# Four-head and half-array TensorE products rewritten as products on the whole array, in a hybrid decoder step

## The chip, the cores and the metric

The kernel runs as one program on one core of a Trainium2 chip. The metric is device time of one execution in microseconds (us); the kernel before has a median of 2491.27 us over three runs (2490.3 to 2497.3).

## The reference

One inference step of a two-layer trunk over 560 token columns: 8 sample sequences of 4 tokens, 16 meta tokens and 512 prompt tokens, model width 1024, all in float32. Per layer:

```python
x = x + 0.5 * swiglu(rmsnorm(x, ffn1_norm), ...)          # 1024 -> 2*2816 -> 1024
h = rmsnorm(x, mix_norm);  parts = split(h @ w_mix_in)
fox  : 4 heads x 64, q/k rmsnorm, logits + F_q - F_k (F = cumsum of log forget gates), softmax
ssd  : conv + silu, 8 heads x 64, 2 groups of B/C; y = (C.B * exp(seg)) x + C h exp(cs)
gla  : 4 heads, key 32, value 64; glog = log_sigmoid(glr @ w_gate + bias) / 16
       att[t,s] = sum_k q[t,k] k[s,k] exp(b[t,k] - b[s,k]);  o = att v + (q exp(b)) S
x = x + concat(fox, ssd, gla) @ w_mix_out
x = x + 0.5 * swiglu(rmsnorm(x, ffn2_norm), ...)
```

The new keys, values, log forget gates and states are outputs too.

## The kernel before

Activations lie with features on the 128 partitions and tokens along the columns, in two groups: A (304 columns: 48 sample and meta tokens as tile 4, prompt tiles 0 and 1) and B (256 columns: prompt tiles 2 and 3). Large products are done in three float32r products of split operands (`mm3`: high by high, high by low, low by high); in the profile these are the matmuls with `hhi`, `hlo` or `hid` and `whi`, `wlo` or `keep`. Weights come in 512 KB pieces (`raw`), ScalarE rounds them to `whi`, VectorE (or now and then GpSimd) takes the rest as `wlo`. Products in plain float32 stand in the trace as two matmul records each.

Each layer runs FFN1, the mixing stage (`mix`), FFN2. In the mixing stage `MIX_ORDER` names the steps in the order of issue, and a scheduler in the language's tile framework lays them side by side: the projections (`fox_in`, `gla_in`, `ssd_in`, `out`) fill TensorE (PE) while the small steps of the head groups (`gla_tile`, `ssd_tile`, `fox_tile`, `fox_decode`, `fox_meta`, `fox_norm`) run between them. PE takes its instructions strictly in the order that the scheduler wrote.

The steps that the change touches:

- `gla_tile` (five tiles a layer) computes the decayed attention by levels: products between the two halves of a block of 128, of 64, of 32, 16 and 8 tokens. The four heads have 32 key rows each, so a head's product contracts over 32 of the 128 partitions (`zk[hr, ...]`, `zq[hr, ...]`). Heads are looped over; every head takes a PSUM bank, and its results go into `att` by ScalarE copies (two coarse levels) and by `copy_predicated` under a mask (three fine levels).
- `ssd_tile`: C by B (`gm`) and C by state (`pi`) are done for each of two groups on 64 of the partitions; the decay sums `pd` on 64 columns.
- `fox_norm`: each token tile's running sum of log forget gates is a product with 4 output rows, chained from tile to tile through `lsum`.
- `fox_tile`: the 16 meta keys are their own 16-row transpose (`femt`) and 16-row product with `Vm`; for the last tile, whose 528 keys don't fit a bank, the scores are cut 16 + 512.
- `gla_in`: the low-rank gate goes tile by tile through a 16-row transpose and a product that contracts over 16 rows.
- `norm`: eight squares; GpSimd adds the first seven, and two one-column products with `ones` for each token tile add the last.

Of the kernel before, what the change touches and what calls it, by code (L numbers as in the profile page):

```python
# [76 lines left out]
TM = [("gv", [(C_GV, 256), (C_GLR, 16)]), ("fv", [(C_FV, 256), (C_FF, 4)]),  # L77
# [9 lines left out]
def constants():  # L87
# [14 lines left out]
    same = seq[:, None] == seq[None, :]  # L102
    put("ident", np.eye(128))
# [4 lines left out]
    put("tri4", same & (t4[:, None] <= t4[None, :]))  # L108
# [11 lines left out]
    put("bd", (P // 32)[:, None] == (np.arange(256) // 64)[None, :])  # L120
    put("fsel", np.where((P // 64)[:, None] == np.arange(2)[None, :], 1.0 / 64, 0.0))
# [104 lines left out]
class Trunk:  # L226
# [108 lines left out]
    def setup_rest(self):  # L335
# [37 lines left out]
        self.Vm = self.t([16, 256], "Vm", pool=self.pers)  # L373
# [3 lines left out]
    def layer_params(self, l, pc=None):  # L377
# [7 lines left out]
        wg = self.t([16, 128], "wgate", pool=self.pers)  # L385
        nc.sync.dma_start(out=wg, in_=a["wgate"][l])
# [44 lines left out]
    def first_norm(self, g, gain):  # L431
# [19 lines left out]
        for j, (_, o, tn) in enumerate(tiles):  # L451
            for i in range(2):
                self.mm(ps[:tn, j:j + 1], acc[i][:, o:o + tn], self.c("ones")[:, 0:1], start=i == 0, stop=i == 1)
        r = self.norm_factors(ps, tiles)
        y = self.ps(pool)[:, :n]
        for j, (_, o, tn) in enumerate(tiles):
            self.tr(y[:, o:o + tn], r[:tn, j:j + 1].to_broadcast([tn, 128]))
# [4 lines left out]
    def norm_factors(self, ps, tiles):  # L462
        r = self.t([128, 2, 3], "nr", bufs=2, pool=self.tmp)
        nt = len(tiles)
        if nt == 3:
            self.V.memset(r[:, 0, 0:1], 1.0)
            self.V.tensor_scalar(r[:48, 0, 0:1], ps[:48, 0:1], 1.0 / D, EPS, op0=ALU.mult, op1=ALU.add)
        self.V.tensor_scalar(r[:, 0, nt - 2:nt], ps[:, nt - 2:nt], 1.0 / D, EPS, op0=ALU.mult, op1=ALU.add)
        return self.rpow(r[:, 0, :nt], r[:, 1, :nt])

    def norm(self, g, gain, order=range(8)):
# [13 lines left out]
        for j, (_, o, tn) in enumerate(tiles):  # L485
            self.mm(ps[:tn, j:j + 1], acc[:, o:o + tn], self.c("ones")[:, 0:1], stop=False)
            self.mm(ps[:tn, j:j + 1], sq[:, o:o + tn], self.c("ones")[:, 0:1], start=False)
        r = self.norm_factors(ps, tiles)
        y = self.ps(pool)[:, :n]
        for j, (_, o, tn) in enumerate(tiles):  # L490
            self.tr(y[:, o:o + tn], r[:tn, j:j + 1].to_broadcast([tn, 128]))
# [115 lines left out]
    def fox_in(self, l, H):  # L607

        for g in GRP:
# [3 lines left out]
            if g == "A":  # L613
                self.G.memset(R["lf"], 0.0)
                self.G.memset(R["fst"], 1.0)

        def use(g):
            def f(j, ti, c0, tn, ps):
                self.act(self.Vt[ti], ps[:tn, 0:256])
                if ti == 4:  # L620
                    self.act(self.Vm, ps[32:48, 0:256])
# [10 lines left out]
        for name in ("fk0", "fk1", "fq0", "fq1"):  # L632
# [4 lines left out]
            for g in GRP:  # L637
# [7 lines left out]
                for j, (ti, c0, tn) in enumerate(TILES[g]):  # L645
                    o = 8 * j + i + (24 if g == "B" else 0)
                    self.mm(pst[:tn, o:o + 2], sq[:, c0:c0 + tn], self.c("fsel"))
        for g in GRP:
            fst, o = self.R[g]["fst"], 24 if g == "B" else 8
            if g == "A":  # L650
                self.V.tensor_scalar(fst[:48, 0, :], pst[:48, 0:8], EPS, None, op0=ALU.add)
            nt = len(TILES[g])
            self.V.tensor_scalar(fst[:, nt - 2:nt, :], pst[:, o:o + 16].rearrange("p (j i) -> p j i", j=2), EPS, None, op0=ALU.add)

    def gla_in(self, l, g, H):
        R, n, nt = self.R[g], GRP[g][1], len(TILES[g])
        gin = self.g2(128 * nt).rearrange("p (j c) -> p j c", j=nt)
        if nt == 3:
            self.G.memset(gin[:, 0, :], 0.0)

        def use(j, ti, c0, tn, ps):
            gv = R["gv", ti] = self.t([128, 256], f"gv{j}")[:tn]
            self.act(gv, ps[:tn, 0:256])
            glr[j] = self.t([128, 16], "glr", bufs=3)[:tn]
            self.act(glr[j], ps[:tn, 256:272])

        glr = {}
        self.tok_unit(l, 0, g, H, use)
        for j, (ti, c0, tn) in enumerate(TILES[g]):
            pt = self.ps(self.psg)  # L670
            self.tr(pt[:16, :tn], glr[j])
            gt = self.t([16, 128], "glrT")
            self.act(gt[:, :tn], pt[:16, :tn])
            pg = self.ps(self.psg)
            self.mm(pg[:tn, :128], gt[:, :tn], self.wgate)
            self.tt(gin[:tn, j, :], pg[:tn, :128], self.row["gb"][:tn], ALU.add)
# [94 lines left out]
    def fox_norm(self, l, g):  # L771
# [7 lines left out]
        for j, (ti, c0, tn) in enumerate(tiles):  # L779
            e = self.f2(512)[:tn]  # L780
            self.act(e.rearrange("p (h d) -> p h d", h=8), y[:tn, j, :].unsqueeze(2).to_broadcast([tn, 8, 64]))
            ps = self.ps(self.psF)
            for i in range(4):
                self.tr(ps[:, i * tn:(i + 1) * tn], e[:, 128 * i:128 * i + 128])
            for h2 in range(2):
                pv = ps[64 * h2:64 * h2 + 64, :4 * tn].rearrange("p (a b t) -> p a b t", a=2, b=2)
# [12 lines left out]
        for j, (ti, c0, tn) in enumerate(tiles):  # L799
            lf = R["lf"][:tn, j, :]  # L800
            tri = self.c("tri") if tn == 128 else self.c("tri4")
            ps = self.ps(self.psF)
            self.mm(ps[:4, :tn], lf, tri[:, :tn], stop=ti == 4)
            if ti < 4:
                self.mm(ps[:4, :tn], self.lsum, self.c("ones")[:, :tn], start=False)
            fr = self.t([4, 128], "frow")
            self.act(fr[:, :tn], ps[:4, :tn], scale=-1.0)
            self.nc.sync.dma_start(out=self.kaug[64:65, :, c0g + c0:c0g + c0 + tn], in_=fr[:, :tn])
            if ti == 4:
                self.V.memset(self.lsum, 0.0)  # L810
                self.V.tensor_copy(self.lsum[32:48], lf[32:48])
            elif ti < 3:
                self.tt(self.lsum, self.lsum, lf, ALU.add)
# [18 lines left out]
    def fox_tile(self, g, i, c0):  # L832
# [3 lines left out]
        cut = 16 if kc + 16 > 512 else 0  # L836
        po = self.ps(self.psF)
        for hp in range(2):
            ets = []
            for h in (2 * hp, 2 * hp + 1):  # L840
                q = self.qaug[:, h, GRP[g][0] + c0:GRP[g][0] + c0 + 128]
                s = self.ps(self.psF)
                nk = kc + 16 - cut
                if cut:
                    sm = self.ps(self.psF)
                    self.mm(sm[:, 0:16], q, self.kaug[:, h, 32:48])
                self.mm(s[:, :nk], q, self.kaug[:, h, 32 + cut:48 + kc], stop=False)
                self.mm(s[:, nk - 128:nk], self.c("ident_b"), self.c("cmask_r"), start=False)
                sums = self.t([128, 2], "fsum", bufs=4)
                e = self.softmax_rows([s[:, :nk]] + ([sm[:, 0:16]] if cut else []), sums)  # L850
                if cut:
# [4 lines left out]
                em = e[1] if cut else e[0][:, 0:16]  # L856
                ek = e[0] if cut else e[0][:, 16:]
                pt = self.ps(self.psF)
                for k in range(i + 1):
                    self.tr(pt[:, 128 * k:128 * k + 128], ek[:, 128 * k:128 * k + 128])  # L860
# [5 lines left out]
                self.act(emt, pm[:16, :128]) if h % 2 else self.V.tensor_copy(emt, pm[:16, :128])  # L866
# [599 lines left out]
```

## Time and profile before

| | us |
|---|---|
| median of three runs | 2491.27 |
| the profiled execution | 2489.21 |
| its span (first to last instruction) | 2487.4 |
| PE busy | 2423.8 (97%) |
| VectorE (DVE) busy | 1243.0 (50%) |
| ScalarE (ACT) busy | 878.5 (35%) |
| GpSimd (POOL) busy | 505.5 (20%) |
| mean granted TensorE clock | 0.975 |

PE's busy time is a model: matmuls are pipelined, and a record lasts longer than the time after which the next one starts. So for PE the distance between starts is read, not the length of a record. "x12" in a timeline row is twelve records merged. The granted clock is 1.0 (2.4 GHz) or 0.5 (1.2 GHz) at any moment. The mixing stages lie at about 430 to 880 us and 1680 to 2090 us.

### The profile page before, as it was taken

What the parts mean: (1) busy time and instruction counts of PE and PEld (TensorE: products, weight loads), DVE (VectorE), ACT (ScalarE), POOL (GpSimd) and SP (SyncE); (2) the same over time, 40 slices, a digit from 0 to 9 for tenths busy, and PEclk for the clock granted to TensorE, in tenths of its full rate; (3) what the DMA queues carried; (4) which work ended last, traced back from release to release, by engine and by line L of the source; (5) the groups of instructions that cost most, each with busy time, mean ns of one, the idle gap of its engine ahead of it and who ended that gap; (6) DMA issues with size and microseconds to landing.
All of it is one profiled execution on the core that took longest, in us unless ns stands there. A gap on an engine that the chain in (4) does not pass through costs nothing. (4 is left out here: it accounts for less than half of the span.)

```text
span 2487.4 us, 45892 instructions
## 1 busy us (share of the span) xinstructions
PE 2423.8 (97%) x18346; PEld 2293.9 (92%) x18346; DVE 1243.0 (50%) x2747; ACT 878.5 (35%) x1990; POOL 505.5 (20%) x675
## 2 busy tenths in 40 slices
PE   8999999999999999999999999999999999999999
PEld 7999999987777899999999999999876779999999
DVE  5434344487687633333343333343867875333333
ACT  4323233444354432322333232334444544323221
POOL 3202124131232310110131010132322323101010
PEclk8999999998898999999999999999989999999999
DMA  4222223353331322222322222223523313222222
GB/s 148 87 88 87 90 84 88 106 146 96 98 95 53 115 69 85 87 86 88 98 67 85 87 86 86 83 90 105 156 87 106 94 58 110 86 85 85 86 86 87
DMA packets 89463, 230.61 MB, mean 93 GB/s; under 512 B 12482, under 2 KB 37826, under 8 KB 89250
## 3 DMA queue, kind: packets, MB, share of 16 engines
q1 hardware_dynamic: 88818, 227.53, 29.3%
q8 instruction: 144, 2.36, 0.4%
q14 instruction: 69, 0.57, 0.1%
q10 hardware_dynamic: 432, 0.16, 0.0%
HBM read 219.71 MB, written 7.92 MB: 92 GB/s over the span
## 5 line engine op out<-in xcount | busy, mean ns | idle before, releaser
L270 DVE TENSOR_TENSOR wlo<-raw,whi 128x512 fp32r<-128x512 f32 (+1 forms) x649 | 464.5, 720 | 404.1 <-ACT whi L276 395.8
L276 ACT ACTIVATE whi<-raw 128x512 fp32r<-128x512 f32 (+1 forms) x680 | 426.6, 630 | 657.7 <-PE ps L263 609.8
L263 PE MATMUL ps<-hhiA,wlo 128*128 128x304 f32 x1664 | 510.8, 307 | 0.0
L263 PE MATMUL ps<-hloA,whi 128*128 128x304 f32 x1664 | 510.2, 307 | 0.0
L263 PE MATMUL ps<-hhiA,whi 128*128 128x304 f32 x1664 | 510.0, 306 | 0.0
L263 PE MATMUL ps<-hhiB,wlo 128*128 128x256 f32 x1664 | 473.0, 285 | 2.4 <-DVE wlo L270 2.4
L263 PE MATMUL ps<-hhiB,whi 128*128 128x256 f32 x1664 | 472.1, 284 | 3.1 <-ACT s L276 2.5
L263 PE MATMUL ps<-hloB,whi 128*128 128x256 f32 x1664 | 470.6, 283 | 0.0
L263 PEld LDWEIGHTS ps<-hhiB,whi 128*128 128x128 f32 x1664 | 316.8, 190 | 7.7 <-ACT s L276 3.4
L263 PEld LDWEIGHTS ps<-hhiA,wlo 128*128 128x128 f32 x1664 | 316.7, 190 | 6.3 <-issue 4.7
L263 PEld LDWEIGHTS ps<-hhiB,wlo 128*128 128x128 f32 x1664 | 316.9, 190 | 5.1 <-DVE wlo L270 3.0
L263 PEld LDWEIGHTS ps<-hhiA,whi 128*128 128x128 f32 x1664 | 316.4, 190 | 4.9 <-issue 3.5
L263 PEld LDWEIGHTS ps<-hloA,whi 128*128 128x128 f32 x1664 | 317.3, 191 | 3.4 <-issue 2.4
L263 PEld LDWEIGHTS ps<-hloB,whi 128*128 128x128 f32 x1664 | 316.4, 190 | 1.7 <-issue 1.2
L270 POOL TENSOR_TENSOR hidA<-s,hidA 128x304 fp32r<-128x304 f32 x88 | 76.4, 868 | 849.3 <-ACT hidA L276 849.2
L263 PE MATMUL ps<-hidA,whi 128*128 128x304 f32 x1072 | 226.2, 302 | 0.0
L273 DVE SCALAR_TENSOR_TENSOR x<-ps,x 128x304 f32<-128x304 f32 (+1 forms) x192 | 85.9, 449 | 232.4 <-PE ps L263 230.6
L263 PE MATMUL ps<-hidB,whi 128*128 128x256 f32 x1072 | 195.2, 282 | 0.0
L263 PEld LDWEIGHTS ps<-hidA,whi 128*128 128x128 f32 x1072 | 174.4, 188 | 0.0
L263 PEld LDWEIGHTS ps<-hidB,whi 128*128 128x128 f32 x1072 | 166.3, 189 | 0.0
L270 DVE TENSOR_TENSOR s<-s,ps 128x256 f32<-128x256 f32 (+3 forms) x194 | 90.4, 466 | 149.5 <-PE ps L263 141.6
L263 PE MATMUL ps<-hidA,wlo 128*128 128x304 f32 x536 | 162.1, 302 | 0.0
(338 smaller groups left out, 3606.2 us busy)
## 6 DMA issues: line engine op xcount, KB each, us to landing
raw<-win SPq DMA_DIRECT2D x176, 512.0 KB, 3.3
raw<-wout SPq DMA_DIRECT2D x64, 512.0 KB, 3.5
raw<-wfm SPq DMA_DIRECT2D x48, 512.0 KB, 3.6
raw<-wmo SPq DMA_DIRECT2D x32, 512.0 KB, 3.6
raw<-wout SPq DMA_DIRECT2D x32, 384.0 KB, 3.7
pg<-kpage SPq DMA_DIRECT2D x64, 130.0 KB, 2.4
pg<-vpage SPq DMA_DIRECT2D x64, 128.0 KB, 2.3
raw<-wtm SPq DMA_DIRECT2D x8, 544.0 KB, 3.8
```

The lines of the kernel that those rows point to most:

```text
L263: return self.T.matmul(out, lhsT, rhs, start=start, stop=stop, **k)
L270: return (eng or self.V).tensor_tensor(out=out, in0=a, in1=b, op=op)
L273: return self.V.scalar_tensor_tensor(out=out, in0=a, scalar=s, in1=b, op0=op0, op1=op1)
L276: return self.S.activation(out, in_, f, **k)
```

## The change

Small products are padded or stacked to use all 128 rows and, where it can be, all 128 columns. For the levels of `gla_tile`, the four heads' q is laid side by side with zeros outside its own 32 rows (`qm`, from `hsel`), so one product over 128 rows with 512 columns gives all four heads in one bank; `qm` and one of the level operands are made on GpSimd, the others on VectorE. The masked copies then take four heads at once. `ssd_tile` does the same for two groups (`scz`, from `gsel`). Norms, forget sums, gates and meta keys use whole tiles, and the last square of a norm is now added by VectorE. The last FoX tile is cut 400 + 128. Pools change: `g2` 5 to 8 buffers, `pg` (cache pages) 12 to 10.

```diff
-ON_POOL = ["gdq1", "gpr3", "gqk", "gzq2", "sr1", "sst", "sy"]
-BUFS = {"s1": 5, "f2": 3, "g2": 5, "s2": 5, "pg": 12}
+ON_POOL = ["gqm", "gdq1", "gpr3", "gqk", "gzq2", "sr1", "sst", "sy"]
+BUFS = {"s1": 5, "f2": 3, "g2": 8, "s2": 5, "pg": 10}
...
 norm:
-            elif i < 7:
-                self.tt(acc[:, :n], acc[:, :n], sq[:, :n], ALU.add, self.G)
+            else:
+                self.tt(acc[:, :n], acc[:, :n], sq[:, :n], ALU.add, self.G if i < 7 else self.V)
-            self.mm(ps[:tn, j:j + 1], acc[:, o:o + tn], self.c("ones")[:, 0:1], stop=False)
-            self.mm(ps[:tn, j:j + 1], sq[:, o:o + tn], self.c("ones")[:, 0:1], start=False)
+            self.mm(ps[:, j:j + 1], acc[:, o:o + 128], self.c("ones")[:, 0:1])
...
 fox_norm (was five tiles, each chained through lsum):
+        self.mm(ps[:, 0:128], lw[:, 0, :], self.c("tri"), stop=False)
+        self.mm(ps[:, 0:48], lw[:, 2, :], self.c("tri4"), start=False, stop=False)
+        self.mm(ps[:, 0:128], lw[:, 1, :], self.c("ones"), start=False)
...
 fox_tile:
-                self.tr(pm[:16, :128], em)
-                emt = self.t([16, 128], "femt", bufs=2)
+                self.tr(pm[:, :128], e[0][:, 0:128])
+                emt = self.t([128, 128], "femt", bufs=2)
...
 ssd_tile:
-            self.mm(pg[:n, :n], bT[pr, cs], cT[pr, cs])
-            self.tt(gm[:, g2, :], pg[:n, :n], tri[:, :n])
+        self.tt(cz, cT[:, cs].unsqueeze(1).to_broadcast([128, 2, n]), self.c("gsel").unsqueeze(2).to_broadcast([128, 2, n]), eng=self.e("scz"))
+        self.mm(pg[:n, :2 * n], bT[:, cs], cz.rearrange("p g t -> p (g t)"))
-                self.mm(pi[:n, 0:256], cT[pr, cs], self.Ssd[pr, :])
+                self.mm(pi[:, 256 * g2:256 * g2 + 256], cz[:, g2, :], self.Ssd)
...
 gla_tile:
-            zq, zk = times(e[:, 0:w], q, f"gzq{lv[-1]}"), times(e[:, 0:w], k, f"gzk{lv[-1]}")
-            for h in range(4):
-                    self.mm(pa[:64, 0:64], zk[hr, 0:64], zq[hr, 64:128])
-                        self.mm(pa[b:b + 32, 64:96], zk[hr, o:o + 32], zq[hr, o + 32:o + 64])
-                        self.mm(pa[:n, ms], zk[hr, ms], zq[hr, ms])
-                        V.copy_predicated(out=att[:, h, :], mask=masks["lev"][:, m, :], data=pa[:n, i * n:(i + 1) * n])
+        self.tt(qm, q.unsqueeze(1).to_broadcast([128, 4, n]), self.c("hsel").unsqueeze(2).to_broadcast([128, 4, n]), eng=self.e("gqm"))
+            self.mm(pa[:, 0:256], zk[:, 0:n], z0)
+            self.mm(pa[:, 256:512], zk[:, n:2 * n], z1)
+            self.tt(zq.rearrange("p (h t) -> p h t", h=4), z.unsqueeze(1).to_broadcast([128, 4, n]), qm, eng=self.e(f"gzq{i}"))
+            self.mm(pa[:n, :4 * n], kk, zq)
+            V.copy_predicated(out=att, mask=masks["lev"][:, i, :].unsqueeze(1).to_broadcast([n, 4, n]),
+                              data=pa[:n, :4 * n].rearrange("p (h t) -> p h t", h=4))
```

The first place is PE in the first layer, at the levels of prompt tile 1 of `gla_tile` (`g` by `g` are level products, `pg` by `f` cache values in `fox_decode`, `hhiA` and `hloA` a projection). Before, three of the four heads at the coarse levels:

```order
L263 MATMUL ps_7028<-g_1135_7015,g_1136_7017 64x64
L263 MATMUL ps_7028<-g_1135_7015,g_1136_7017 32x32 x2
L263 MATMUL ps_7028<-g_1135_7015,g_1136_7017 128x128
L263 MATMUL ps_6992<-c_hsel_652,gpr_7079 128x4 x2
L263 MATMUL ps_7434<-hloA_4664,whi_7430 128x304
L263 MATMUL ps_7037<-g_1135_7015,g_1136_7017 64x64
L263 MATMUL ps_7037<-g_1135_7015,g_1136_7017 32x32 x2
L263 MATMUL ps_7037<-g_1135_7015,g_1136_7017 128x128
L263 MATMUL ps_6992<-c_hsel_652,gpr_7079 128x4
```

And now, on the same engine, the whole tile's levels:

```order
L265 MATMUL ps_6941<-g_1122_6942,g_1120_6939 128x256
L265 MATMUL ps_6941<-g_1123_6945,g_1120_6939 128x256
L265 MATMUL ps_6593<-pg_6649,f_995_6587 32x256
L265 MATMUL ps_6593<-pg_6647,f_995_6587 32x256
L265 MATMUL ps_6593<-pg_6645,f_995_6587 32x256
L265 MATMUL ps_6593<-pg_6643,f_995_6587 32x256
L265 MATMUL ps_6954<-g_1124_6952,g_1120_6939 128x512
L265 MATMUL ps_6961<-g_1127_6959,g_1126_6957 128x512
```

A head's four products, in three shapes, have become a share of a few products that all fill the array.

The second place is PE at the end of the first layer's mixing stage, where the norm of group B sums its squares (`c_ones` by `s`) and FFN2 begins on group A (`hhiA` by `keep`). Before:

```order
L263 MATMUL ps_10058<-hhiB_9634,wlo_10055 128x256
L263 MATMUL ps_10106<-c_ones_82,s_1852_10084 128x1
L263 MATMUL ps_10183<-hhiA_9906,keep_10175 128x304
L263 MATMUL ps_10183<-hloA_9907,keep_10175 128x304
L263 MATMUL ps_10183<-hhiA_9906,keep_10176 128x304
```

And now; the last product of the mixing stage's output (`hhiB` by `wlo`) stands seventeen rows ahead of the first of these, with FFN2 products on `hhiA` and `hloA` alone in between:

```order
L265 MATMUL ps_9971<-hloA_9695,keep_9967 128x304
L265 MATMUL ps_9971<-hhiA_9694,keep_9968 128x304
L265 MATMUL ps_9971<-hhiA_9694,keep_9967 128x304
L265 MATMUL ps_9971<-hloA_9695,keep_9967 128x304
L265 MATMUL ps_9895<-c_ones_82,s_1819_9872 128x1 x2
L265 MATMUL ps_9971<-hhiA_9694,keep_9968 128x304
L265 MATMUL ps_9971<-hhiA_9694,keep_9967 128x304
```

The sum of squares has moved behind twenty products of FFN2.

## Rows read from the trace of the kernel before

**Rows 1.** The page, sections 1 and 2: busy time by engine, and the granted clock in tenths.
```profile
PE 2423.8 (97%) x18346; PEld 2293.9 (92%) x18346; DVE 1243.0 (50%) x2747; ACT 878.5 (35%) x1990; POOL 505.5 (20%) x675
...
PEclk8999999998898999999999999999989999999999
```

**Rows 2.** Stretches: from:to, length, busy (instructions) by engine, clock, DMA share, GB/s.
```profile
430.00:880.00 450.00, 428.83 (x3067) 364.31 (x3065) 304.78 (x794) 194.97 (x524) 125.03 (x193) 0.91 0.32 98
880.00:1680.00 800.00, 796.20 (x6168) 794.22 (x6167) 304.06 (x552) 243.03 (x473) 113.01 (x135) 1.00 0.27 85
1680.00:2090.00 410.00, 387.81 (x2882) 327.18 (x2883) 299.74 (x780) 189.52 (x512) 120.90 (x182) 0.96 0.35 105
```

**Rows 3.** Timeline of PE: one head's coarse levels between projection products (start, us, what).
```profile
720.81 0.28 PE L263 MATMUL ps<-hhiB,wlo 128*128 128x256 f32 x1
721.02 0.92 PE L263 MATMUL ps<-g,g 32*64 32x64 f32 x8
721.87 0.39 PE L263 MATMUL ps<-whi,hhiB 128*128 128x256 f32 x1
722.09 0.28 PE L263 MATMUL ps<-wlo,hhiB 128*128 128x256 f32 x1
```

**Rows 4.** Timeline of PE: fine levels, three heads together and one head alone.
```profile
561.58 0.73 PE L263 MATMUL ps<-g,g 32*128 32x128 f32 x12
...
1806.58 0.71 PE L263 MATMUL ps<-g,g 32*128 32x128 f32 x4
1807.22 0.40 PE L263 MATMUL ps<-hhiA,whi 128*128 128x304 f32 x1
```

**Rows 5.** Timeline of PE: a float32 product of full height with 400 columns.
```profile
1997.90 0.30 PE L263 MATMUL ps<-hhiA,wlo 128*128 128x304 f32 x1
1998.03 0.83 PE L263 MATMUL ps<-kaug,qaug 128*128 128x400 f32 x2
1998.71 0.22 PE L263 MATMUL ps<-c_cmask_r,c_identb 128*128 128x128 bf16 x1
```

**Rows 6.** Timeline of PE: projection products between half-height products.
```profile
1988.76 0.41 PE L263 MATMUL ps<-hhiA,whi 128*128 128x304 f32 x1
1989.00 0.30 PE L263 MATMUL ps<-hloA,whi 128*128 128x304 f32 x1
1989.23 0.70 PE L263 MATMUL ps<-Ssd,xc 64*128 64x256 f32 x2
```

**Rows 7.** Four of the stretches with the lower granted clock (columns as in rows 2).
```profile
584.40:598.00 13.60, 13.60 (x56) 10.48 (x55) 7.42 (x26) 4.45 (x14) 0.40 (x2) 0.50 0.14 41
...
772.10:785.80 13.70, 13.00 (x61) 9.77 (x60) 6.11 (x21) 3.71 (x16) 1.25 (x2) 0.50 0.00 1
843.80:854.00 10.20, 9.67 (x39) 9.48 (x40) 4.58 (x12) 3.98 (x10) 3.00 (x5) 0.50 0.35 113
1826.80:1840.50 13.70, 13.70 (x59) 10.54 (x59) 7.08 (x25) 3.98 (x14) 0.57 (x4) 0.50 0.13 41
```

**Rows 8.** Timeline of PE at the end of the first layer's mixing stage.
```profile
844.33 0.59 PE L263 MATMUL ps<-c_ones,s 128*128 128x1 f32 x2 [2.74 <-POOL s L270]
844.78 0.60 PE L263 MATMUL ps<-hhiA,keep 128*128 128x304 f32 x1
```

**Rows 9.** Groups by line and shape, VectorE: busy us, mean ns, idle before.
```profile
L1205 DVE COPY_PREDICATED g<-c_lev_r,ps 128x128 f32<-128x128 uint8 x96 | 25.3, 294 | 13.5 <-PE ps L263 6.9 <-ACT g L276 6.4
L1222 DVE COPY_PREDICATED g<-c_band_r,gdb 128x512 f32<-128x512 uint8 x24 | 17.8, 743 | 0.0
L270 DVE TENSOR_TENSOR s<-c_tri,dr 128x512 fp32r<-128x512 f32 x16 | 14.0, 875 | 1.9 <-PE ps L263 1.9
L270 DVE TENSOR_TENSOR g<-g,gq 128x384 f32<-128x384 f32 x8 | 4.6, 574 | 0.0
```

**Rows 10.** The same for GpSimd.
```profile
L270 POOL TENSOR_TENSOR s<-s,prow 128x512 f32<-128x512 f32 x8 | 10.9, 1364 | 30.6 <-ACT s L276 30.6
L270 POOL TENSOR_TENSOR g<-g,gq 128x256 f32<-128x256 f32 x8 | 7.0, 877 | 4.6 <-DVE g L270 4.6
```

More of the change, by code (lines that the diff above doesn't have):

```diff
@@ L102, in constants @@
     same = seq[:, None] == seq[None, :]
+    pad = lambda a: np.concatenate([a, np.zeros((80,) + a.shape[1:], bool)], 0)
     put("ident", np.eye(128))
@@ L452, in first_norm @@
             for i in range(2):
-                self.mm(ps[:tn, j:j + 1], acc[i][:, o:o + tn], self.c("ones")[:, 0:1], start=i == 0, stop=i == 1)
+                self.mm(ps[:, j:j + 1], acc[i][:, o:o + 128], self.c("ones")[:, 0:1], start=i == 0, stop=i == 1)
         r = self.norm_factors(ps, tiles)
@@ L464, in norm_factors @@
         nt = len(tiles)
[L465 to L468, printed above, removed]
+        self.V.tensor_scalar(r[:, 0, :nt], ps[:, :nt], 1.0 / D, EPS, op0=ALU.mult, op1=ALU.add)
         return self.rpow(r[:, 0, :nt], r[:, 1, :nt])
@@ L798, in fox_norm @@
         self.nc.sync.dma_start(out=self.a["olf"][l, o:o + 256].rearrange("(j p) h -> p j h", p=128), in_=R["lf"][:, j0:j0 + 2, :])
[L799 to L813, printed above, removed]
+        if g == "A":
+            return
+        lw = self.f2(384).rearrange("p (i c) -> p i c", i=3)
+        self.G.memset(lw, 0.0)
+        lfA, lfB = self.R["A"]["lf"], R["lf"]
+        self.V.tensor_copy(lw[:, 0, 0:8], lfA[:, 1:3, :].rearrange("p j h -> p (j h)"))
+        self.V.tensor_copy(lw[:, 0, 8:16], lfB[:, 0:2, :].rearrange("p j h -> p (j h)"))
+        self.V.tensor_copy(lw[:48, 2, 16:20], lfA[:48, 0, :])
+        self.V.tensor_copy(lw[32:48, 1, 0:4], lfA[32:48, 0, :])
+        for j in range(3):
+            self.tt(lw[:, 1, 4 * j + 4:4 * j + 8], lw[:, 1, 4 * j:4 * j + 4], lw[:, 0, 4 * j:4 * j + 4], ALU.add)
+        ps = self.ps(self.psF)
+        self.mm(ps[:, 0:128], lw[:, 0, :], self.c("tri"), stop=False)
+        self.mm(ps[:, 0:48], lw[:, 2, :], self.c("tri4"), start=False, stop=False)
+        self.mm(ps[:, 0:128], lw[:, 1, :], self.c("ones"), start=False)
+        fr = self.t([20, 128], "frow")
+        self.act(fr, ps[:20, 0:128], scale=-1.0)
+        for ti in range(5):
+            o, tn = (0, 48) if ti == 4 else (48 + 128 * ti, 128)
+            self.nc.sync.dma_start(out=self.kaug[64:65, :, o:o + tn], in_=fr[4 * ti:4 * ti + 4, :tn])
     def softmax_rows(self, ps_list, sums):
@@ L835, in fox_tile @@
         kc = 128 * (i + 1)
-        cut = 16 if kc + 16 > 512 else 0
+        nk = kc + 16 if kc + 16 <= 512 else kc - 112
         po = self.ps(self.psF)
@@ L1009, in ssd_tile @@
         self.mm(ps[:n, 8:16], strict[:, :n], da)
+        if not last:
+            self.mm(ps[:, 16:24], self.c("ones"), da)
         E1 = self.t([128, 16], "sE1", bufs=2)[:n]
@@ new lines, in gla_tile @@
+        for i in range(2 if last else 3):
+            if last:
+                z, kk = eb[:, i * n:(i + 1) * n], zk[:, i * n:(i + 1) * n]
+            elif i == 0:
+                z, kk = ea[:, 3 * n:], zk[:, 2 * n:3 * n]
+            else:
+                if i == 1:
+                    zk = times(eb[:, 0:2 * n], k, "gzk2")
+                z, kk = eb[:, (i - 1) * n:i * n], zk[:, (i - 1) * n:i * n]
+            zq = self.g2(4 * n)
+            self.tt(zq.rearrange("p (h t) -> p h t", h=4), z.unsqueeze(1).to_broadcast([128, 4, n]), qm, eng=self.e(f"gzq{i}"))
+            pa = self.ps(self.psL)
+            self.mm(pa[:n, :4 * n], kk, zq)
+            V.copy_predicated(out=att, mask=masks["lev"][:, i, :].unsqueeze(1).to_broadcast([n, 4, n]),
+                              data=pa[:n, :4 * n].rearrange("p (h t) -> p h t", h=4))
```

151 lines of the change are left out of this document (73 added, 78 removed).

## The prediction, made before the change was run

> **What bounds the kernel now.** I read the page first: PE is busy 97% of the span, VectorE half of it, and the granted clock is at its upper level in all but a few slices [rows 1]. Then the span in three stretches [rows 2]. Between 880 and 1680 us (the FFNs) PE takes 800 us with weights loading for 794 of them: back to back, with nothing to win for this change. In the two mixing stages, 450 and 410 us long, weights load for only 364 and 327 us, VectorE rises to 305 of 450 and 300 of 410, and the mean clock falls to 0.91 and 0.96 [rows 2]. So about 86 + 83 = 169 us of the two stages pass in which PE loads no weights, and of them the change can win a part. Of that, the clock: a mean of 0.91 over 450 us is 2 x 0.09 x 450 = 81 us at 1.2 GHz, and 0.96 over 410 us 33 us; together 114 us at half speed, worth at most 57 us.
>
> Last the timelines of PE. A steady projection product starts 0.13 us after the one before [rows 5]. A change of the product's tile shape shows as a longer step: 0.24 us from the first projection product after a half-height product to the next, and 0.23 us from that one to the next half-height product [rows 6], about 0.1 us extra each. A change of shape is the thing that the small products cost and that no busy share shows. In the order of the built program, neighbours on PE differ in tile shape 689 times before and 322 times now; 162 of the 689 lie beside a level product over 32 rows, and none do now.
>
> **The sum, part by part**, against the profiled execution's own 2489.2 us (the span of 2487.4 and 1.8 around it), 2.1 us under the median.
>
> *Levels of the GLA tiles, eight full tiles in two layers.* One head's coarse levels, alone between projection products, take from 720.81 to 722.09 us, 1.28 us; without two projection steps of 0.13 us each that is 1.02 us, and four heads 4.1 us [rows 3, 5]. The fine levels take 0.73 us for three heads and 0.64 us for a lone one, 1.4 us together [rows 4]. So a tile costs up to 5.5 us; where heads follow each other the changes of shape between them are shared, and one record's length has a tail in it, so the lower bound is 4.8 us. Now a tile has three products of 512 columns and two of 256. A full-height product of 400 columns takes 0.68 us to the next start [rows 5]; by columns, 512 are 0.87 us and 256 0.44 us: 3 x 0.87 + 2 x 0.44 = 3.5 us. I take 5.2 - 3.5 = 1.7 us a tile, **-14 us** over eight (bounds -10 and -16 from the two costs; the meta and sample tile breaks about even). These costs hold the 162 changes of shape.
>
> *The other changes of shape.* 689 - 162 - 322 = 205 fewer, in the SSD groups, meta keys, norms, gates and forget sums, at 0.09 us, a shade under the two steps of [rows 6]: **-18 us**. Bounds: 0, if a wait lies under each of them, and -21 at 0.1 us.
>
> *Fewer products.* 25 of the 60 one-column sums of squares go, beside eight decay sums and most of the forget chain. One such product, two records, takes 0.45 us at half clock [rows 8], so some 0.2 us at full: -5 us for the norms. The wide SSD products replace as much as they add. **-5 us**, between 0 and -9.
>
> *The norm at the end of the mixing stage.* PE stands for 2.74 us at the first sum of squares of group B, with all of FFN2's first products queued behind it, until GpSimd has added the squares [rows 8]. In the new order some twenty projection products, 20 x 0.13 = 2.6 us [rows 5], stand in front of it. The wait goes for the most part, in two layers: **-5 us**. What is late next is VectorE's extra addition, which now comes after both ScalarE's last square and GpSimd's sum; with nothing in front of it it would cost its own half microsecond, as a 384-column product does with 0.574 us [rows 9], in each of six norms: +3 us is the other end.
>
> *The clock.* Three of the lower stretches, 13.6, 13.7 and 13.7 us, have level products over 32 rows before or in them, and one of 10.2 us follows the wait at the norm [rows 7, 8]. Together 51 us at 1.2 GHz, a loss of 26 us. What PE did before the fall is thin products or standing; what replaces them is full products, and one wait less. I take two thirds, **-17 us**. Bounds: -57 us, were the clock never to fall, and +7 us, were one more stretch of 13.7 us to come in behind a new wait.
>
> *Operand work that hides or doesn't.* VectorE loses, per tile, twelve masked copies at 0.294 and one product at 0.574 us, 4.1 us; it gets three masked copies at 0.743 us, two 512-wide products at 0.875 us and three narrow ones at no more than 0.574 us, 5.7 us at most [rows 9]. So up to +1.6 us a tile, +13 us in all, against 145 idle microseconds in the first stage and 110 in the second [rows 2]. GpSimd gets the masked q at 1.364 us and pays 0.49 us more for its level operand, +1.9 us a tile [rows 10]. Both lie beside PE's projection work, and I cost them at nothing; uncovered they are the last rival below.
>
> The Trainium skill, "GPSIMD Engine Reference" (the table at its head), says that GpSimd shares its SBUF interfaces with VectorE and contends with VectorE's instructions that read two SBUF inputs. Masked operands are such instructions on both engines. No run here isolates it; by that rule the 13 and 15 us above would lengthen each other, still under the idle time.
>
> Terms: 14 + 18 + 5 + 5 + 17 = 59 us. Not all of it reaches the end: PE that comes earlier meets waits that other engines set, and VectorE is busy two thirds of the first stage and nearly three quarters of the second [rows 2]. I give back a quarter, 15 us. 2489.2 - 44 = 2445 us, and 2 us for the median: **2447 us**.
>
> **Rivals.**
>
> *Small products ran side by side.* For it: twelve records of three heads' fine levels pass in 0.73 us [rows 4], a quarter of what twelve would take one after another at the 0.34 us of a 400-column record [rows 5], more than their columns explain. If heads mostly ran so, a tile would cost about 2 us (eight fine products at 0.12 us and sixteen smaller ones at 0.06 us) and now 3.5: +12 us in place of -14. Time 2447 + 26 = 2473 us. Against it: a lone head's coarse levels take 1.02 us [rows 3], and heads stand apart in the order. The Trainium skill's "TensorEngine Tiling (Array Packing)", Theoretical Speedup, promises up to 4 times for dimensions of 32 or less, and by that rule this change gives away what the array can do; the rows show both cases.
>
> *The clock does not move and the waits eat the rest.* The lows may come from the decode's narrow products, from half-height products and from standing, which stay in part. Without the 17 us: 2464 us.
>
> *The clock hardly falls.* 45 of the 57 us in place of 17: 2419 us. For it: the second stage already runs at 0.96 with the same program [rows 2].
>
> *Nothing reaches the end.* VectorE, at 300 of 410 us in the second stage, takes over as the bound there and gives all back: 2491 us. Against it: 110 us of idle time.
>
> *Slower: PE stands at each wide operand.* Place: the five products of each full GLA tile, which now wait for operands that are four times as wide, the last of them on GpSimd. Uncovered, a tile's operands take three narrow ones at up to 0.574, two at 0.875 and one at 1.364 us, 4.8 us [rows 9, 10]: 39 us over eight tiles. If a stand of that length brings a 10.2 us stretch at half clock, as the one of 2.74 us at the norm did [rows 7, 8], that is 5.1 us each, 41 us. Against them stand 42 us without the clock term: 2491 - 42 + 80 = 2529 us. It decides from about half of the 80 us on. Against it: the operands depend on the gates and on masked q alone, not on each other, and eight `g2` buffers let them be made ahead.
>
> **How the numbers follow.** The forecast (2432 to 2463 us by itself) has 0.46; packed products 0.12; the clock unmoved 0.12; the clock nearly free 0.15; nothing gained 0.06; slower 0.09. The range runs from the freer clock's lower end, 2412, to 2480 us, where the packed case with its own spread ends; outside it lie nothing-gained, slower, and a little of the free clock. A difference of 0.3%, some 7.5 us, is what can be told from no change: faster 0.85, same 0.06, slower 0.09.
>
> **What would show it.** In the profile after: no `g` by `g` product over 32 rows, and products of 512 columns that start 0.87 us before the next at full clock. Weight loading in the mixing stages shorter by little, the stages themselves shorter by some 20 us each. The wait of `c_ones` on GpSimd at the first stage's end gone or under 1 us. A mean clock near 0.94 in the first stage. POOL busy some 15 us more, ACT less. The prediction is wrong if PE's list of waits shows the level products waiting for `g` on VectorE or GpSimd for tens of microseconds, if the stages keep their length with the shapes gone (then changes of shape were not what took the time), or if the FFN stretches change.

## The result and the profile after

The changed kernel takes 2455.66 us (median of 4 runs, 2449.21 to 2456.21), the kernel before 2494.28 us over 4 runs: a ratio of 0.984, 95% interval [0.982, 0.986]. In another series of runs, on another chip, it was 2457.87 against 2496.68 us, 0.985 [0.982, 0.987]. The forecast was 2447 us, 44 us less than the 2491 it knew; 39 us came.

The changed kernel's page, sections 1 and 2, answers to [rows 1]:

```profile
span 2453.5 us, 44862 instructions
PE 2368.8 (97%) x17908; PEld 2254.9 (92%) x17908; DVE 1256.3 (51%) x2675; ACT 869.7 (35%) x1902; POOL 523.7 (21%) x688
PEclk9999999989899999999999999999899999999999
```

Three things can be read from this page and that of before. The span is 33.9 us shorter. PE's time without a product, span less PE's busy time, was 2487.4 - 2423.8 = 63.6 us and is 2453.5 - 2368.8 = 84.7: **21 us more standing**. The mean granted clock was 0.975 and is 0.986. If a stretch at half speed took twice as long, a mean clock c would cost (1 - c) of the time: 62 us before, 34 us now, **28 us less**. What is left, 33.9 + 21 - 28 = 27 us, would be **PE's own work**: products and changes of shape.

The 28 us are an upper bound, since half speed takes somewhat less than twice the time here. In the kernel before, a projection product starts 0.14 us after the last one at full clock and 0.25 us after it at half:

```profile
769.01 0.30 PE L263 MATMUL ps<-hhiA,whi 128*128 128x304 f32 x1
769.15 0.30 PE L263 MATMUL ps<-hloA,whi 128*128 128x304 f32 x1
...
1831.79 0.46 PE L263 MATMUL ps<-hhiA,wlo 128*128 128x304 f32 x1
1832.04 0.46 PE L263 MATMUL ps<-hhiA,whi 128*128 128x304 f32 x1
```

And over 40 runs of the kernel before (18, 11 and 11 in the three series of the experiments) a line through time and mean clock falls by 2.1 us for each 0.001 of clock, where (1 - c) gives 2.5. By that line some 24 of the 28 us are the clock's, and 31 us PE's own.

The stretches, cut where the same projection products begin. First the kernel before (length, busy time and count by engine, clock, DMA share, GB/s), then the changed one:

```profile
434.20:860.00 425.80, 404.63 (x2869) 340.18 (x2869) 299.38 (x783) 189.56 (x512) 121.19 (x188) 0.91 0.33 101
860.00:1677.00 817.00, 813.72 (x6308) 812.07 (x6307) 307.94 (x557) 247.19 (x481) 114.22 (x132) 1.00 0.27 85
1677.00:2085.50 408.50, 385.78 (x2870) 324.82 (x2869) 298.38 (x781) 189.09 (x511) 122.01 (x188) 0.96 0.34 104
```

```profile
431.30:834.60 403.30, 371.15 (x2663) 316.14 (x2662) 304.10 (x748) 185.19 (x468) 131.21 (x195) 0.95 0.35 107
834.60:1649.50 814.90, 811.60 (x6291) 810.28 (x6290) 309.86 (x557) 247.47 (x481) 113.53 (x132) 1.00 0.28 85
1649.50:2051.70 402.20, 367.53 (x2663) 311.65 (x2661) 305.58 (x748) 184.12 (x467) 132.10 (x193) 0.97 0.35 107
```

The gain lies in the mixing stages, 22.5 us in the first and 6.3 in the second. The first stage's clock rose from 0.91 to 0.95 (by (1 - c) 38 us lost to it before, 20 now): up to 18 of its 22.5 us. In both stages PE's standing grew, in the first from 21 to 32 us and in the second from 23 to 35 (length less PE's busy time).

Four long half-clock stretches of before were 13.6, 13.7, 10.2 and 13.7 us [rows 7]. There was a fifth of that length, without a level product in it or near it: PE works there on products over 48 and 16 rows (`s` by `sbm`, `wgate` by `glrT`) between projection products.

```profile
639.00:652.70 13.70, 13.70 (x44) 9.43 (x45) 6.47 (x20) 2.95 (x9) 0.00 (x0) 0.50 0.25 84
```

In the changed kernel's profile none is longer than 6.8 us (in that of its repetition one is 10.2). Two that now stand in the first layer:

```profile
645.00:651.80 6.80, 5.57 (x24) 5.00 (x25) 3.03 (x8) 1.98 (x7) 2.25 (x4) 0.50 0.25 77
...
825.90:829.30 3.40, 3.12 (x14) 2.86 (x13) 2.13 (x6) 2.77 (x7) 1.61 (x3) 0.50 0.85 275
```

Of the 14 half-clock stretches in the mixing stages of before, 7 had level products over 32 rows shortly ahead of them; there are 11 now, and no such product exists. By the timeline of PE (start, length, what, in brackets what it waited for) these two stand beside waits:

```profile
642.74 0.28 PE L265 MATMUL ps<-hhiB,whi 128*128 128x256 f32 x1
646.23 0.42 PE L269 MATMUL ps<-c_ident,s 48*128 48x48 f32 x2 [3.21 <-DVE s L1136]
...
818.02 0.28 PE L265 MATMUL ps<-hhiB,wlo 128*128 128x256 f32 x1
819.47 0.38 PE L265 MATMUL ps<-hhiA,keep 128*128 128x304 f32 x1 [1.17 <-issue]
...
824.40 0.61 PE L265 MATMUL ps<-c_ones,s 128*128 128x1 f32 x4 [1.91 <-DVE s L272]
```

The last two answer to [rows 8]. The one wait of 2.74 us on GpSimd at the end of the first mixing stage has become two: 1.17 us before FFN2's first product, for which the row names no engine, and 1.91 us on VectorE's added sum, 3.1 us in all. The twenty products that were to cover it did start earlier, and PE ran out of them.

PE's waits by releaser (total us, times, longest), the first rows of the changed kernel:

```profile
PE ps L265 <- DVE s L272: 10.6, 10, 2.1
PE ps L269 <- DVE s L1136: 9.6, 7, 3.2
PE ps L265 <- ACT s L278: 7.7, 17, 2.4
```

GpSimd's `s`, with 10.0 us the first of these rows in the kernel before, is down to 1.6; VectorE's `s` leads. Before the level products PE waited 1.3 us in the kernel before (third number of these groups):

```profile
L263 PE MATMUL ps<-g,g 32*128 32x128 f32 x192 | 33.3, 375 | 0.9 <-DVE g L1205 0.9
L263 PE MATMUL ps<-g,g 32*64 32x64 f32 x64 | 10.8, 249 | 0.4 <-DVE g L270 0.2
L263 PE MATMUL ps<-g,g 128*48 128x64 f32 x32 | 3.7, 231 | 0.5 <-DVE g L270 0.5
```

And in the changed kernel 6.4 us (2.7 + 2.8 + 0.9):

```profile
L265 PE MATMUL ps<-g,g 128*128 128x512 f32 x48 | 25.4, 619 | 2.7 <-DVE g L272 2.1 <-POOL lfr L949 0.6
L265 PE MATMUL ps<-g,g 128*128 128x256 f32 x32 | 9.2, 393 | 2.8 <-ACT s L278 1.7 <-DVE g L272 0.9
L265 PE MATMUL ps<-g,g 128*48 128x64 f32 x32 | 4.4, 265 | 3.2 <-issue 3.2
L265 PE MATMUL ps<-g,g 128*48 128x192 f32 x8 | 2.4, 386 | 0.9 <-DVE g L272 0.9
```

The row of 128x64 in both is no level product: it is the meta and sample tile's product with the samples' states, which the change leaves alone. Its wait grew from 0.5 to 3.2 us (run 1 below, with the old levels, has 2.1), and the 9.6 us that some expectations below put before level products count it in.

### The profile page after: what moved, and what is told of

Its sections match the earlier page's. It is cut to its first block, busy times and chain, and to the rows that moved or that the text cites. A ratio compares the mean times of both kernels' runs of the same rounds, so it can differ in the third digit from the quotient of the medians.

```text
span 2453.5 us, 44862 instructions
## 1 busy us (share of the span) xinstructions
PE 2368.8 (97%) x17908; PEld 2254.9 (92%) x17908; DVE 1256.3 (51%) x2675; ACT 869.7 (35%) x1902; POOL 523.7 (21%) x688
```

## The experiments

Two theories: (1) the forecast's, that products and changes of shape go and the rest hides; (2) that waits eat the products' gain and the time saved is that of the clock. The runs came in three series on different chips (1 to 4; 5 to 8; 9 to 11 and the repetition), and the kernel before took 2494.95, 2499.5 and 2496.68 us in them, so kernels are compared by their ratio to before in their own series. The **full-clock time** in the table is each run's time multiplied by its mean clock, the median over the runs; for before it is 2427.2, 2427.0 and 2426.7 us in the three series. It counts (1 - c) of the time as the clock's, which the result section found to be too much by some 15%; by 2.1 us for each 0.001 of clock (the smaller rate, below) the full-clock times would be 2437 us for before, 2426 for changed, 2426 for run 1, 2442 for run 2, 2441 for run 3 and 2433 for run 11. Single runs of one kernel differ by up to 12 us in it. The idle time is span less PE's busy time in one profile; the expectations count it between products only, without the 9.4 us at the start and the end, so that 63.6 and 84.7 us are 54 and 75 there.

| kernel | median us | ratio [95%] | clock | full-clock us | PE idle us |
|---|---|---|---|---|---|
| before | 2494.95 | 1 | 0.973 | 2427.2 | 63.6 |
| changed, first / repeated | 2455.66 / 2457.87 | 0.984 / 0.985 [0.982, 0.987] | 0.986 / 0.987 | 2420.2 / 2421.4 | 84.7 / 84.5 |
| 1 changed, levels as before | 2478.26 | 0.994 [0.992, 0.996] | 0.975 | 2415.9 | 74.4 |
| 2 before, levels wide | 2478.24 | 0.993 [0.991, 0.996] | 0.983 | 2435.3 | 76.8 |
| 3 before, levels full height | 2484.14 | 0.997 [0.995, 0.999] | 0.980 | 2433.6 | 66.8 |
| 4 changed, norms as before | 2461.79 | 0.986 [0.984, 0.989] | 0.986 | 2426.2 | 86.8 |
| 5 changed, operands left out | 2446.39 | 0.979 [0.977, 0.980] | 0.983 | 2405.4 | 73.4 |
| 6 changed, SSD as before | 2467.58 | 0.988 [0.986, 0.989] | 0.981 | 2419.5 | 80.3 |
| 7 changed, keys as before | 2470.64 | 0.989 [0.987, 0.990] | 0.981 | 2423.7 | 82.7 |
| 8 changed, gates as before | 2461.31 | 0.985 [0.983, 0.986] | 0.984 | 2422.1 | 83.3 |
| 9 changed, last operand on VectorE | 2449.25 | 0.981 [0.979, 0.984] | 0.986 | 2413.9 | 80.8 |
| 10 changed, both on VectorE | 2450.21 | 0.982 [0.979, 0.984] | 0.986 | 2416.4 | 87.0 |
| 11 as 1, levels full height | 2464.62 | 0.988 [0.985, 0.990] | 0.984 | 2427.8 | 77.9 |

**1, the changed kernel with its levels per head.**

```diff
-            self.mm(pa[:n, :4 * n], kk, zq)
+                        self.mm(pa[:n, ms], zk[hr, ms], zq[hr, ms])
```

> The changed kernel with the GLA level products per head again, as before (masked q gone too); everything else changed. Its order has 445 changes of tile shape against 322. Theory 1, the prediction's: the levels' own PE time comes back, 5.2 - 3.5 = 1.7 us a tile, 14 us over eight tiles, and two thirds of the 20 us of clock that stood at level products, 13.6 us, less a quarter given back: 21 us slower than the changed kernel, about 2476 us, with the half-clock time in the first mixing stage back from 37 to some 65 us. Theory 2, waits eat the products' gain and only the clock reaches the end: slower by half of the half-clock time that comes back and by nothing else, and PE's idle time falls from 75 toward 54 us. Rival, levels hardly matter: within 7 us of the changed kernel, 2455 to 2462 us.

**2, the kernel before with wide levels alone**: the same edit the other way round.

> The kernel before with the wide GLA level products and masked q alone (and the changed buffer counts), nothing else changed. 559 changes of tile shape against 689. Theory 1: 21 us faster than before, about 2472 us. Theory 2: the time falls by half of the half-clock time that goes and by no more, and PE's idle time rises by some 10 us because its operands are wide now. Rival, the gain needs the other parts: within 7 us of before.

The two agree. Undone, the levels' change costs 0.9%, some 23 us, near theory 1's 21; alone it brings 17 us. But the full-clock time says what it is made of. Without the wide levels the changed kernel would be up to 5 us *faster* at full clock (2415.9 against 2420.2 and 2421.4; level with it by 2.1 us for each 0.001); with them alone the kernel before is 8 us *slower* (2435.3 against 2427.2; 5 by the smaller rate). The whole gain of the levels is clock: 0.975 to 0.986, and 0.973 to 0.983. Theory 2 holds here: the waits of PE took all that the products gave. In the profiles PE's idle time is 10 us longer with the wide levels than in run 1 (84.7 against 74.4) and 13 us longer in run 2 than before (76.8 against 63.6).

**3, the kernel before, levels per head on the whole array.**

```diff
-                    self.mm(pa[:64, 0:64], zk[hr, 0:64], zq[hr, 64:128])
+                    self.mm(pa[:, 0:64], zk[:, 0:n], zq[:, 64:128])
```

> The kernel before with its level products still one per head and as many, of as many columns, but with all 128 rows and 128 weight columns in each, so that no product is a small tile. It leaves out the separation of heads: each product sums over all four heads. 548 changes of tile shape against 689, and VectorE, ScalarE and GpSimd do what they did before. If a change of tile shape costs 0.09 us whatever else is done: 141 x 0.09 = 13 us faster, 2481 us, with the products themselves at 24 a tile x two records x 0.11 us = 5.3 us, what they took before. If the level products' gain is only that there are fewer of them: no faster than before, within 7 us. If thin products were what drew the clock down: the half-clock time in the first mixing stage falls from 78 to below 50 us and the time by another 14 us. If the small products ran side by side: about 12 us slower, 2506 us.

The first mixing stage, 430 to 880 us as in [rows 2], in run 1, in run 3 and in run 11, which follows:

```profile
430.00:880.00 450.00, 420.87 (x3065) 364.58 (x3064) 309.18 (x789) 195.94 (x520) 127.66 (x195) 0.93 0.33 99
```

```profile
430.00:880.00 450.00, 428.77 (x3175) 373.60 (x3174) 311.78 (x803) 199.19 (x532) 128.09 (x196) 0.95 0.33 100
```

```profile
430.00:880.00 450.00, 418.57 (x3212) 374.21 (x3211) 318.82 (x801) 202.53 (x533) 134.31 (x197) 0.98 0.33 103
```

By these clocks 2 x 0.07 x 450 = 63 us of the stage ran at half clock in run 1, as expected there, 45 us in run 3 against 81 in the kernel before [rows 2], and 18 us in run 11. In the second mixing stage the clock rises by 0.01 only, from 0.96 to 0.97 and from 0.95 to 0.96.

**11, the same in the kernel of run 1.** As in run 3, its products leave out the separation of heads.

> The changed kernel with the level products per head as before, but with all 128 rows and weight columns in each (24 products a full tile, no wide operands). It leaves out the separation of heads. 323 changes of tile shape against 445 with the small products and 322 in the changed kernel. If the clock falls because of products on a small part of the array: half-clock time falls from the 122 us of the per-head small products toward the changed kernel's 70 us and the time by some 20 us. If merging heads is what matters (fewer, wider products): half-clock time stays above 110 us and the time within 8 us of the per-head small products.

Neither run has fewer products, nor other work on any engine but PE. At full clock both are slower than what they replace, by 6 us (2433.6 against 2427.2) and 12 us (2427.8 against 2415.9; 4 and 8 by the smaller rate). Some 3 us of each are standing (idle 66.8 against 63.6, 77.9 against 74.4). Counted from start to next start at full clock, with waits left out, the level products take 47 us in run 3 against 44 before, and 47 in run 11 against 46 in run 1. So small products did run side by side in part, as a rival had it, but in the kernel before that is worth 3 of its 12 us; where the rest of run 11's loss lies was not found. And the clock rises from 0.973 to 0.980 and from 0.975 to 0.984, so both are faster, run 3 by 0.3% and run 11 by 0.6%, some 15 of the 20 us expected. Two stretches around level products, chosen where run 1's clock was low, in run 1 and then in run 11:

```profile
560.00:600.00 40.00, 39.62 (x257) 27.98 (x255) 25.41 (x76) 16.52 (x53) 8.64 (x20) 0.72 0.44 139
740.00:780.00 40.00, 38.86 (x222) 31.53 (x221) 28.36 (x68) 15.17 (x47) 7.59 (x9) 0.79 0.20 57
```

```profile
560.00:600.00 40.00, 38.90 (x314) 31.28 (x313) 31.40 (x93) 18.00 (x59) 9.69 (x19) 0.98 0.39 119
740.00:780.00 40.00, 37.13 (x266) 31.25 (x263) 33.54 (x79) 19.85 (x61) 11.31 (x12) 1.00 0.19 59
```

PE is busy for 97 to 99% of the time in run 1 and 93 to 97% in run 11; with small products the clock is 0.72 and 0.79, with about as many full ones 0.98 and 1.00. So what the levels' change brings to the clock is that its products have the full shape, not that there are fewer of them. One rival is not ruled out: full products also need fewer changes of shape (689 to 548 in run 3, 445 to 323 in run 11), and no run changes the one without the other. Run 4 below, with 36 changes more at the same clock, speaks against the changes alone, but does not settle it.

**4, the changed kernel with the old norms.**

```diff
-                self.tt(acc[:, :n], acc[:, :n], sq[:, :n], ALU.add, self.G if i < 7 else self.V)
+            elif i < 7:
+                self.tt(acc[:, :n], acc[:, :n], sq[:, :n], ALU.add, self.G)
```

> The changed kernel with the norms as before (GpSimd adds all but the last square, two one-column products per tile, the 48-row tile small). 358 changes of tile shape against 322. Theory 1, the prediction's: 5 us of products, 5 us of the wait at the stage's end, 3.4 us of clock and 36 x 0.09 = 3.2 us of shapes come back, less a quarter: 12 us slower than the changed kernel, about 2468 us. Theory 2: the two traces show the wait at the end of each mixing stage moved, not gone (2.74 us on GpSimd before, 1.9 us on VectorE and 1.2 us on ScalarE now), so the norm's change is worth its products alone: 0 to 5 us slower, 2455 to 2460 us.

The ratio is 0.2% higher, with intervals that overlap; by the medians 4 to 6 us, by the full-clock time 5 to 6 us, at the same clock. That is theory 2's 0 to 5 us and half of theory 1's 12: the products that went count, the wait does not. Before sums of squares and before FFN2's products of `hhiA` by `keep` PE stands for 11 us with the old norms and for 12 with the new (without the first wait of the program).

**6, 7 and 8, the SSD groups, the forgetting attention's keys and sums, and the GLA gates as before**, each in the changed kernel. One line of each:

```diff
-                self.mm(pi[:, 256 * g2:256 * g2 + 256], cz[:, g2, :], self.Ssd)
+                self.mm(pi[:n, 0:256], cT[pr, cs], self.Ssd[pr, :])
...
-        self.mm(ps[:, 0:128], lw[:, 0, :], self.c("tri"), stop=False)
+            self.mm(ps[:4, :tn], lf, tri[:, :tn], stop=ti == 4)
...
-            self.mm(pg[:, 128 * j:128 * j + 128], gt[:, 128 * j:128 * j + 128], self.wgate)
+            self.mm(pg[:tn, :128], gt[:, :tn], self.wgate)
```

> The changed kernel with the SSD groups as before (half-height products with the state and for C by B, two decay products apart). 380 changes of tile shape against 322. Theory 1, the prediction's: 58 x 0.09 = 5 us come back, and the wide products replace as much as they add: 5 us slower than the changed kernel, about 2460 us. Theory 2: no time of its own, only the clock, which does not depend on these: within 4 us of 2455. Rival: the half-height products ran side by side (two records of 256 columns from state to state in less than their columns take one after another), so undoing it is faster, 2448 to 2453 us.

> The changed kernel with the forgetting attention's parts as before: meta keys in products of their own, head sums and forget sums per tile, 16- and 48-row tiles. 412 changes of tile shape against 322. Theory 1: 90 x 0.09 = 8 us and some 3 us of products come back: 11 us slower than the changed kernel, 2466 us, less what PE finds waiting anyway (a third). Theory 2: half-clock time as in the changed kernel (68 us), time within 5 us of it.

> The changed kernel with the GLA gate products per tile as before (16-row products, a transpose of 16 rows each). 348 changes of tile shape against 322. Theory 1: 26 x 0.09 = 2.3 us and about 2 us of products: 4 us slower than the changed kernel, 2459 us. Theory 2: no change that can be measured.

SSD and keys cost 0.3% and 0.4% when undone, some 9 and 11 us; the gates cannot be told from nothing, and SSD's interval [0.986, 0.989] still overlaps the changed kernel's [0.982, 0.987]. At full clock that is -1, +3 and +1 us, within the spread of single runs: again clock for the most part (0.981 against 0.986 for the first two), which the expectation that it "does not depend on these" had wrong. The losses of clock when one part is undone, 26 us for the levels, 12 and 11 for SSD and keys (median less full-clock time, against 36), add to more than the 34 that the whole change gained in the series that had both kernels (70 - 36): they are not independent.

**5, the wide operands left out.**

```diff
-            zq = self.g2(4 * n)
-            self.tt(zq.rearrange("p (h t) -> p h t", h=4), z.unsqueeze(1).to_broadcast([128, 4, n]), qm, eng=self.e(f"gzq{i}"))
+            zq = qm.rearrange("p h t -> p (h t)")
```

> The changed kernel with the wide operands of the level products left out: the products read masked q alone, so the gates are not multiplied into q; per full GLA tile VectorE loses two products of 512 and three narrow ones, GpSimd one of 512 (35 and 11 us in all). PE's products and their order stay. If the 21 us by which PE's idle time rose (54 to 75 us) come from this operand work: idle falls to about 60 us or below and the time by 12 to 20 us, to 2440 us or less. If PE only comes earlier to waits that other work sets (theory 2): idle stays within 5 us of 75 apart from the level products' own 4 us of waiting, and the time within 7 us of the changed kernel's 2455.

It took 9 to 12 us off the time and 15 us off the full-clock time, and PE's idle time fell by 11 us, half of it the wait before level products (6.4 to 0.7). VectorE's products that went are 25 us by their groups in the changed kernel's trace, not the 35 of the expectation. The larger products no longer wait:

```profile
L265 PE MATMUL ps<-gqm,g 128*128 128x512 f32 x48 | 25.0, 612 | 0.3
L265 PE MATMUL ps<-gqm,g 128*128 128x256 f32 x32 | 8.8, 393 | 0.1
```

So the operand work sets about half of the 21 us of new standing, a quarter of it directly at level products; the other half is there without it, and neither bound of the expectation was met in full.

**9 and 10, where the operand is made.** In the changed kernel VectorE's product of 512 columns takes 0.68 us alone, and 1.76 us when GpSimd's own masked product runs beside it:

```profile
705.88 0.68 DVE L272 TENSOR_TENSOR g<-g,gqm 128x512 f32<-128x512 f32 x1
```

```profile
578.27 1.76 DVE L272 TENSOR_TENSOR g<-g,gqm 128x512 f32<-128x512 f32 x1
```

```profile
578.09 1.39 POOL L272 TENSOR_TENSOR g<-g,gqm 128x512 f32<-128x512 f32 x1 [1.37 <-DVE g L272]
```

```diff
-ON_POOL = ["gqm", "gdq1", "gpr3", "gqk", "gzq2", "sr1", "sst", "sy"]
+ON_POOL = ["gqm", "gdq1", "gpr3", "gqk", "sr1", "sst", "sy"]
```

> The changed kernel with the last wide operand of each full tile (512 columns) made on VectorE instead of GpSimd, the masked q still on GpSimd. In the changed kernel's trace VectorE's own 512-column operand takes 0.68 us alone and 1.75 us where GpSimd's runs beside it, and GpSimd's takes 1.42 us. Theory A, the two engines held each other up and the level products stand for it: PE's wait before level products falls from 9.6 us to 6 or less, and the time by 3 to 8 us against the changed kernel in the same call. Theory B, PE would have waited anyway: time within 3 us, the wait only moves to other products. Theory C, VectorE is too full in these stages: slower by 3 to 6 us (eight times 0.68 us on VectorE).

> The changed kernel with both the last wide operand and the masked q of each tile on VectorE. Theory A: as with one operand moved, and masked q comes in about 0.7 us instead of 1.21: 4 to 10 us faster than the changed kernel. Theory B: within 3 us. Theory C: VectorE has 2 x 8 x 0.7 = 11 us more to do and PE waits for its other work (weight splitting, scaling) instead: slower by up to 8 us.

> The changed kernel itself, for comparison within one call: 2450 to 2460 us, half-clock time 60 to 80 us.

One operand moved (run 9): 2449.25 against 2457.87 us for the changed kernel in the same series, 9 us, and 7 us at full clock. Single runs of the two overlap in time (2445.5 to 2454.6 and 2451.3 to 2460.2), but not at full clock (2411 to 2415 and 2417 to 2426). Both moved (run 10) is no better. In run 9 the wait before the level products fell from 6.4 us (6.9 in the repetition) to 2.5 (0.1 + 1.5 + 0.9), and every product of 512 columns on VectorE now takes about 0.68 us:

```profile
L265 PE MATMUL ps<-g,g 128*128 128x512 f32 x48 | 25.1, 616 | 0.1
L265 PE MATMUL ps<-g,g 128*128 128x256 f32 x32 | 9.4, 395 | 1.5 <-DVE g L272 1.5
L265 PE MATMUL ps<-g,g 128*48 128x64 f32 x32 | 3.5, 230 | 0.2 <-issue 0.2
L265 PE MATMUL ps<-g,g 128*48 128x192 f32 x8 | 2.1, 344 | 0.9 <-DVE g L272 0.9
L272 DVE TENSOR_TENSOR g<-g,gqm 128x512 f32<-128x512 f32 x24 | 15.8, 680 | 1.5 <-PE ps L265 1.5
```

Theory A holds: PE's idle time in the profile fell by 4 us and the time by 7 to 9. Run 9 beats both kernels: 0.981 of before.

## Why the prediction was right, step by step

The time was right, in part by luck, for the sum behind it was not: an error of 16 to 21 us on PE's work and waits and one of 7 to 17 us on the clock, of opposite sign, all but cancelled. (The ranges come from the two rates for the clock, 2.1 and 2.5 us for each 0.001.)

- *The clock, -17 us*: the mechanism held (runs 3 and 11 show it for the levels) and the size was too small: 24 to 28 us in the profiles, 28 to 34 over the runs. I counted only the three stretches with level products in the rows and one at the norm, and took two thirds. Left out were shorter ones and the 13.7 us from 639.00 us on, without level products; undone, the SSD groups and keys lose some 11 us each. The bound of 57 us held it.
- *Levels -14, shapes -18, products -5*: together 37 us of PE's own work; the two pages give 27 to 31. Counted as for run 3, the level products took 44 us before and 33 now: 11 of the 14 us. For the rest of the levels' term the cause is in the trace. I took 0.87 us for a product of 512 columns and 0.88 for two of 256. PE's timeline in the changed kernel:

```profile
577.15 1.10 PE L265 MATMUL ps<-g,g 128*128 128x256 f32 x4 [0.71 <-DVE g L272]
578.18 0.64 PE L265 MATMUL ps<-pg,f 128*32 128x256 f32 x8
...
581.78 1.12 PE L265 MATMUL ps<-g,g 128*128 128x512 f32 x2
582.74 0.51 PE L265 MATMUL ps<-c_hsel,gpr 128*128 128x4 f32 x4
```

From start to next start the two of 256 columns take 1.03 us and one of 512 takes 0.96. A tile is then some 3.9 us, not 3.5, against 4.8 at my lower bound. What one change of shape costs was not measured apart.
- *The norm's wait, -5 us*: failed. What was late next was named, VectorE's addition, at +3 us for all norms, and it took most of the wait's place; a new wait before FFN2's first product took the rest. PE stood 9 us at sums of squares and at products of `hhiA` by `keep` before (without the first wait of the program) and stands 12 now: the other end, +3 us, is what came.
- *Operands at nothing*: failed by half of the new standing, 11 us by run 5. The 5.7 us a tile lie beside projection work, but the last operand and VectorE's second one, made at the same time, held each other up, and PE stood 6.4 us at level products. VectorE's product took 1.76 us there in place of 0.68. The Trainium skill, "GPSIMD Engine Reference" (the table at its head), has the two engines contend for the SBUF interfaces that they share when VectorE reads two SBUF inputs; the trace agrees. I had weighed it under the idle time of VectorE, which is the wrong place: it lengthens the chain that PE waits for.
- *Given back, 15 us*: 21 us of standing came. With the norm's term I had a net 10. The second mixing stage shows it best: it was to be some 20 us shorter and is 6.3, with 12 us more of standing in it.
- The sum without the clock was to be -27 us and was -6 to -11 (profiles: 21 - 27 or 21 - 31; runs: 2427 to 2421 us at full clock, 2437 to 2426 by the smaller rate). "Nothing reaches the end" came nearest for everything but the clock, and it was the rival I gave least; that VectorE is the bound, as it had it, no run shows.
- "Small products ran side by side" is true by some 3 us (run 3); its twelve records in 0.73 us are less than a fifth, not a quarter, of 12 x 0.34 us [rows 4, 5]. "Slower" had its mechanism, PE standing at wide operands, at 6.4 of the 39 us that it named.

Of the 21 us of new standing 5 lie at level products and 11 go with the operand work. Why the other 10 fall where they do was not settled. That PE comes earlier to the same waits is argued, not shown. Nor was it tried whether the half-clock stretches that are left go when the waits beside them go.

## What to carry to other kernels

Split a measured difference into clock and the rest first: time multiplied by the mean clock gave the same number for one program in three series within 0.5 us, where its medians lay 4.5 us apart. Fit the rate to runs of one program before small differences are read from it: here it was 2.1 us for each 0.001, not 2.5. Count what small products cost in the clock, not only in their own time; products of full shape can pay though the kernel loses a little at full clock (runs 3 and 11). And when operands grow wide, ask which engine's instruction runs beside them, since two engines that make parts of the same operand may hold each other up.

## What the runs showed of the hardware that was not expected

- The kernel before, 18 runs in one series: 2476.74 us at a mean clock of 0.981 to 2508.34 us at 0.967. The same program is 31.6 us apart by the clock that it is granted, 2.3 us for each 0.001.
- VectorE and GpSimd, each with a masked product of 512 columns, together: VectorE 1.76 us in place of 0.68 where GpSimd began first. The two overlap by some 1.2 us, and 0.55 of VectorE's remain, so it looks as if they took turns rather than shared. The other pairs of the changed kernel's trace say the same: in all six where GpSimd began first VectorE ends 0.54 to 0.55 us after it, though one of them overlaps by 0.6 us only (VectorE 1.16 us), and in the one where VectorE began first it is GpSimd that takes 1.76 us in place of 1.28 to 1.39:

```profile
1922.57 0.68 DVE L272 TENSOR_TENSOR g<-g,gqm 128x512 f32<-128x512 f32 x1
1922.63 1.76 POOL L272 TENSOR_TENSOR g<-g,gqm 128x512 f32<-128x512 f32 x1 [0.28 <-PE ps L265]
```

The Trainium skill, "Trainium Architecture — The Big Picture" (What this means for kernel authors), calls the shared port an exclusive lock and not a split of bandwidth, and the trace agrees.
- The Trainium skill, "TensorEngine Tiling (Array Packing)", Key Properties, says that a change of tiling mode drains TensorE. The steps in [rows 6] agree; no run here puts a price on one change by itself.
